# Tokens or features on the partitions: which operand of a split matrix product stays and which moves

## The chip, the cores and the metric

The program runs on one core of a Trainium2 chip. The metric is device time in microseconds (us) of one execution. TensorE (PE) multiplies a stationary operand, loaded first, by a moving operand that streams past it, into PSUM; VectorE (DVE), ScalarE (ACT) and GpSimd (POOL) work on tiles in SBUF and PSUM; SyncE (SP) issues nearly all loads of weights. Before the change the median of three runs is 2907.19 us (2906.72 to 2914.02).

## The reference, cut to what matters

256 tokens of width 1024 pass through two stacks, all in float32. First, twice:

```
x = layer_norm(a*x + 0.5*swiglu(x, ffn1_w1, ffn1_w2))     # 1024 -> 2 x 2816 -> 1024
x = layer_norm(a*x + token_mix(x))                        # three attentions, three gates, w_out
x = layer_norm(a*x + 0.5*swiglu(x, ffn2_w1, ffn2_w2))
...
swiglu(x, w1, w2):  gt, up = split(x @ w1);  return (silu(gt) * up) @ w2
token_mix:  g = sigmoid(h @ w_gate + b_gate)              # 1024 -> 3 x 1024
            merged = g0*(o_a @ w_br_a) + g1*(o_b @ w_br_b) + g2*(o_c @ w_br_c)
            return merged @ w_out
```

Then a state-space mixer (SSD) with layer norm, a mixture of 32 experts (two per token, hidden width 512) with layer norm, a dilated attention with layer norm, and a second such mixture with layer norm. That makes ten layer norms.

## The kernel before, in words

**Split products.** A float32 product is made of three fp32r products. Every weight tile of 128 x 1024 is split into a high part (`split`, L82, ACT) and the rest (L83, DVE), and so is the activation; `mm3` (L109 to L112) issues high x high, high x low and low x high. Such weights land in four raw tiles of 1 MB (`wraw`, tag w) and are split into a ring of seven tiles (`whl`, NSPLIT).

**Features on partitions.** x lies as `X["h"]`, `X["l"]` (the split parts) and `X["T"]` (whole), each [128 features, 8 chunks, 256 tokens]. In every split product a block of 128 x 128 weights is the stationary operand and the 256 tokens move, so the product has 128 features on the partitions, 256 tokens along the row.

**Stages.** `ffn` walks over 22 hidden chunks j of 128: `gate_up` projects gate and up (8 chunks of x, 24 products each), the activations are made on ACT and DVE, and `acc_second` adds chunk j - 2 to eight accumulators, four PSUM banks (24 products). `token_mix` projects queries, keys and values, runs attention a, then `branch_gate(0)` and `branch_out(0)`, the same for b and c, and w_out chunk by chunk behind the last branch (`done`). SSD and dilated attention end with an output product in the same form. A list scheduler orders the instructions of each engine: in program order where it can, but a later instruction that is ready fills a gap.

**Layer norm** (`finish`, L211): the last two or three chunks of the accumulation run output chunk by output chunk (`last_chunks`), and behind each of them DVE adds the residual (L230), subtracts a first mean (L234), ACT squares (L238), and PE sums over partitions with matrices of ones (L267, L268). Then follow variance, scale and shift for each chunk (L298 to L309). PE is given products of ones (`warm`, L198: ten of them, 20 records, four in the experts' norm) while it waits. `after_norm` orders the splits behind the norm's work.

**Experts** (`moe`): pairs of experts; tokens are gathered by a product with a selection matrix (L1459), gate and up (L1491) and down (L1527) have 64 gathered tokens stationary in half the columns of the array and 512 weight columns moving, unsplit fp32; the result is added back by L1555, eight products of 256 columns. An unsplit fp32 product of full width makes two records. Weights come straight from HBM into a ring of 21 tiles of 1 MB. The residual enters by products with a scaled unit matrix (L1301), x is turned to tokens on partitions (L1355), and the last pair's norm takes its mean ahead.

**Setup.** Parameter rows (norm weights, gate biases, SSD's) are loaded into three tiles `prow` out of two buffers and turned on PE (L159) during the first FFN.

Of the kernel before, what the change touches and what calls it, by code (L numbers as in the profile page):

```python
# [18 lines left out]
D = 1024  # L19
# [3 lines left out]
ORDER = ("a6 r r r r a5 a4 a3 s s s s s s s a2 a1 a0 x2 x0 x1", "a6 a5 r r r r a4 a3 a2 a1 a0 s s s s s s s x2 x0 x1")  # L23
GROUPED = {c: g for g in ((0, 1, 2, 3, 4, 5),) for c in g}
SETUPJ = (4, 10, 18)
POOLC = (6, 7)
MP, MD = (0, 1, 2, 3), (4, 5, 6)
# [3 lines left out]
WARM = 10  # L31
W2 = 4
W3 = 4
SC2 = 2
DTAIL = 2
F = 2816
# [10 lines left out]
def tile_stack(ctx: ExitStack, tc: tile.TileContext, a: dict, out: bass.AP):  # L47
# [20 lines left out]
    def after_norm(*ins):  # L68

        n = behind.get("n", 99)  # L70
        for k, x in zip(("act", "dve"), ins):
            if n < NSPLIT - TAIL and behind["known"]:
                tc.add_manual_dep(x.ins, behind[k + "0"].ins.name, order, reason="norm")
                if k == "dve":
                    tc.add_manual_dep(x.ins, behind["add0"].ins.name, order, reason="norm")
            elif NSPLIT - TAIL <= n < NSPLIT:
                tc.add_manual_dep(x.ins, behind[k].ins.name, order, reason="norm")
        behind["n"] = behind.get("n", 99) + 1

    def split(w, shape):  # L80
        hi, lo = split_tile(shape)
        after_norm(nc.scalar.activation(out=hi, in_=w, func=AF.Copy),  # L82
                   nc.vector.tensor_tensor(out=lo, in0=w, in1=hi.bitcast(F32), op=ALU.subtract))  # L83
        return hi, lo

    def acc_second(accs, c, n, wh, wl, mh, ml):
        for o in range(KC):
            mm3(accs[o // 2][:, o % 2, :], wh[:, o * 128:(o + 1) * 128], wl[:, o * 128:(o + 1) * 128], mh, ml,
                first=(c == 0 and o % 2 == 0), last=(c == n - 1), skip=True)

    def project_group(tiles, ws):

        for c in range(KC):
            for i, (wh, wl, n) in enumerate(ws):
                mm3(tiles[i // 2][0:n, i % 2, :], wh[:, c], wl[:, c], X["h"][:, c, :], X["l"][:, c, :],
                    first=(c == 0 and i % 2 == 0), last=(c == KC - 1), skip=True)
        return [tiles[i // 2][:, i % 2, :] for i in range(len(ws))]
# [11 lines left out]
    def mm3(o, wh, wl, xh, xl, first, last, skip=False):  # L109
# [10 lines left out]
    ones8 = const.tile([128, 128], F32)  # L120
    nc.vector.memset(ones8, 8.0 / D)

    prow = [
# [10 lines left out]
    pars = const.tile([128, 384], F32)  # L134

    def load_params(pp, pq):
# [6 lines left out]
        for i in range(3):  # L143
# [13 lines left out]
        for i in range(3):  # L157
# [3 lines left out]
        nc.vector.tensor_scalar(out=bg, in0=pars[:, pcol["b_gate"]:pcol["b_gate"] + 48].rearrange("p (l c) -> p l c", l=DEPTH),  # L161
                                scalar1=0.5, scalar2=None, op0=ALU.mult)

# [4 lines left out]
    bg = const.tile([128, DEPTH, 24], F32, name="bg")  # L168
# [5 lines left out]
    def x_tile(key, shape=(128, KC, S), dtype=F32R):  # L174

        return xp.tile(list(shape), dtype, tag="x" + key, name="x" + key)

    def new_x():
        X["h"], X["l"] = x_tile("h"), x_tile("l")
        if "T" not in X:  # L180
            X["T"] = x_tile("T", dtype=F32)
# [13 lines left out]
    def warm(out, n, after):  # L195

        for _ in range(n):
            x = nc.tensor.matmul(out=out, lhsT=ones, rhs=ones8.unsqueeze(1).to_broadcast([128, 2, 128]), start=True, stop=True,  # L198
# [3 lines left out]
    def last_chunks(accs, ks, first):  # L202

        def f(c):
            cs = slice(c * 128, (c + 1) * 128)
            for n, (wh, wl, mh, ml) in enumerate(ks):
                mm3(accs[c // 2][:, c % 2, :], wh[:, cs], wl[:, cs], mh, ml, first=(first and n == 0 and c % 2 == 0),
                    last=(n == len(ks) - 1), skip=True)
        return f

    def finish(accs, last, scale, g, b, write=None, loaded=False, mean=None, side="right"):  # L211

        with pool(name="lnps", bufs=1, space=PSUM, side=None if side else "right") as lps, pool(name="lnr", bufs=1, side=side) as lr, \
                pool(name="lnt", bufs=2, side=side) as tmp:
            rT = lr.tile([128, KC, S], F32, name="rT")  # L220
            st = lps.tile([128, 2, S], F32, name="lnst")
            sv = lps.tile([128, S], F32, name="lnsv")
            if not loaded:
                table("natural_log_exp_and_others")
            end, part, done = None, {}, []
            for c in range(KC):
                acc = accs[c // 2][:, c % 2, :]
                last(c)
                if mean is None:
                    nc.vector.scalar_tensor_tensor(out=rT[:, c, :], in0=X["T"][:, c, :], scalar=ALPHA * scale, in1=acc,  # L230
                                                   op0=ALU.mult, op1=ALU.add)
                    if c == 0:
                        nc.tensor.matmul(out=st[:, 0, :], lhsT=ones8, rhs=rT[:, 0, :], start=True, stop=True)
                    nc.vector.tensor_tensor(out=rT[:, c, :], in0=rT[:, c, :], in1=st[:, 0, :], op=ALU.subtract)  # L234
                else:
                    behind["dve0"] = nc.vector.tensor_tensor(out=rT[:, c, :], in0=acc, in1=mean, op=ALU.subtract)
                sq = tmp.tile([128, S], F32, tag="sq", name="sq", bufs=3)
                behind["act0"] = nc.scalar.activation(out=sq, in_=rT[:, c, :], func=AF.Square)  # L238
                if mean is not None:
                    eng, cs = (nc.gpsimd, MP) if c in MP else (nc.vector, MD if c in MD else (c,))  # L240
                    if c != cs[0]:
                        q2 = tmp.tile([128, S], F32, tag="q2" if c in MP else "r2", name="q2")
                        x = eng.tensor_tensor(out=q2, in0=part[cs], in1=sq, op=ALU.add)  # L243
                        if c in MD:
                            behind["add0"] = x
                        sq = q2
                    part[cs] = sq
                    if c == cs[-1]:
                        end = nc.tensor.matmul(out=sv, lhsT=ones, rhs=sq, start=(not done), stop=(c == KC - 1), skip_group_check=True)  # L249
                        done.append(c)  # L250
                    continue
                if c in GROUPED:
# [1525 lines left out]
```

## Time and profile before

| | |
|---|---|
| median of 3 runs | 2907.19 us |
| the profiled execution's own time | 2909.27 us |
| its span, first to last instruction | 2907.4 us |
| mean granted TensorE clock | 0.990 |
| bytes read from HBM | 693.25 MB |

In the rows below a time at the start of a line is us from the span's start. A line of the timeline shows start, duration, engine, source line, operation, what is written and read, stationary rows x columns, moving shape, and how many equal instructions were merged; what stands in brackets is idle time of the engine before it and what ended it. PE's instructions are pipelined: each is shown for longer than the distance to the next one's start, and that distance is what a product costs in a stream. In such lines a merged group's duration runs to the end of its last product.

### The profile page before, as it was taken

The page shows a single profiled execution, that of the slowest core. Times are in us where ns is not written, and L with a number is a line of the kernel's source. Part 1 is how long each engine was busy: PE and PEld are TensorE (multiplying, and loading weights), DVE is VectorE, ACT ScalarE, POOL GpSimd, SP SyncE. Part 2 cuts the span into 40 slices and gives each one's busy share as a digit, 9 for nine tenths or more (in the row PEclk, how much of TensorE's full clock was granted, in tenths as well). Part 3 has the DMA queues.
Part 4 walks back from the last instruction along what each step waited for, and adds up shares of the span by engine and source line. Part 5 has one row for each costly group of instructions (what it writes and reads, how often), then busy time and mean ns, then how long its engine had stood idle before and what let it go on. Part 6 is the DMA issues. An engine that isn't in the chain of part 4 may idle for free. (4 is left out here: it accounts for less than half of the span.)

```text
span 2907.4 us, 46673 instructions
## 1 busy us (share of the span) xinstructions
PE 2806.7 (97%) x19129; PEld 2194.8 (75%) x19129; DVE 1402.8 (48%) x3051; ACT 1069.7 (37%) x1985; POOL 196.1 (7%) x263
## 2 busy tenths in 40 slices
PE   8899999999999999999999989999998999999998
PEld 8798899999999889999988954445447974444444
DVE  5466665755755756575688741111118752111103
ACT  4344555544544455544467620101015531000002
POOL 2102000200200200020010010000002010000000
PEclk9899999999999999999999999999999999999999
DMA  8765454455455645445545579999956468999992
GB/s 225 194 203 149 134 154 145 145 194 189 155 179 161 179 118 163 145 147 191 167 133 192 220 309 416 421 421 421 421 230 181 132 232 328 421 421 421 421 421 98
DMA packets 312106, 697.45 MB, mean 240 GB/s; under 512 B 19460, under 2 KB 238384, under 8 KB 262736
## 3 DMA queue, kind: packets, MB, share of 16 engines
q1 hardware_dynamic: 300288, 677.62, 63.9%
q10 hardware_dynamic: 9296, 11.66, 1.4%
q0 software_dynamic: 2304, 5.15, 1.2%
q8 instruction: 152, 2.49, 0.4%
q14 instruction: 66, 0.54, 0.1%
HBM read 693.25 MB, written 4.27 MB: 240 GB/s over the span
## 5 line engine op out<-in xcount | busy, mean ns | idle before, releaser
L83 DVE TENSOR_TENSOR whl<-w,whl 128x1024 fp32r<-128x1024 f32 x487 | 591.2, 1220 | 348.8 <-ACT whl L82 343.3
L82 ACT ACTIVATE whl<-w 128x1024 fp32r<-128x1024 f32 x487 | 507.2, 1050 | 355.8 <-PE gu L112 106.6
L110 PE MATMUL pp<-xh,whl 128*128 128x256 f32 x1432 | 417.4, 292 | 9.7 <-DVE cv L935 4.7
L111 PE MATMUL pp<-xl,whl 128*128 128x256 f32 x1432 | 417.9, 292 | 1.1 <-DVE xl L307 1.0
L112 PE MATMUL pp<-xh,whl 128*128 128x256 f32 x1432 | 412.3, 288 | 0.4 <-DVE whl L509 0.4
L110 PE MATMUL gu<-xh,whl 128*128 128x256 f32 x1408 | 400.7, 285 | 4.0 <-DVE h L360 2.6
L112 PE MATMUL gu<-xh,whl 128*128 128x256 f32 x1408 | 400.7, 285 | 0.5 <-DVE whl L83 0.5
L111 PE MATMUL gu<-xl,whl 128*128 128x256 f32 x1408 | 400.8, 285 | 0.1
L110 PEld LDWEIGHTS pp<-xh,whl 128*128 128x128 f32 x1432 | 273.8, 191 | 18.1 <-ACT xh L306 5.7
L111 PEld LDWEIGHTS pp<-xl,whl 128*128 128x128 f32 x1432 | 274.5, 192 | 10.0 <-issue 6.9
L112 PEld LDWEIGHTS pp<-xh,whl 128*128 128x128 f32 x1432 | 274.2, 192 | 4.3 <-issue 2.4
L110 PEld LDWEIGHTS gu<-xh,whl 128*128 128x128 f32 x1408 | 272.0, 193 | 6.3 <-ACT whl L82 3.5
L111 PEld LDWEIGHTS gu<-xl,whl 128*128 128x128 f32 x1408 | 272.2, 193 | 0.8 <-DVE xl L307 0.7
L112 PEld LDWEIGHTS gu<-xh,whl 128*128 128x128 f32 x1408 | 272.1, 193 | 0.8 <-DVE whl L83 0.8
L110 PE MATMUL acc<-hhi,whl 128*128 128x256 f32 x704 | 201.6, 286 | 2.4 <-DVE rT L230 2.2
L111 PE MATMUL acc<-hlo,whl 128*128 128x256 f32 x704 | 200.1, 284 | 1.6 <-issue 1.6
L112 PE MATMUL acc<-hhi,whl 128*128 128x256 f32 x704 | 198.9, 284 | 0.0
L1509 DVE SCALAR_TENSOR_TENSOR t<-t,gps 128x512 f32<-128x512 f32 x32 | 22.0, 687 | 352.7 <-ACT t L187 352.7
L1459 PEld LDWEIGHTS xgp<-ot,xtok 128*128 128x128 f32 x1024 | 120.9, 191 | 50.3 <-issue 24.3
L1459 PE MATMUL xgp<-ot,xtok 128*128 128x128 f32 x1024 | 136.9, 283 | 15.8 <-ACT xg L1442 9.0
L110 PEld LDWEIGHTS acc<-hhi,whl 128*128 128x128 f32 x704 | 135.6, 193 | 5.4 <-DVE rT L230 4.0
L187 ACT ACTIVATE t<-gps 128x512 f32<-128x512 f32 x32 | 19.1, 597 | 320.8 <-PE gps L1491 320.8
(573 smaller groups left out, 4998.7 us busy)
## 6 DMA issues: line engine op xcount, KB each, us to landing
w<-in_ffn_w_dram SPq DMA_DIRECT2D x130, 1024.0 KB, 5.5
wa<-in_moe_w_up_dram SPq DMA_DIRECT2D x45, 1024.0 KB, 11.7
whl<-in_moe_w_down_dram SPq DMA_DIRECT2D x45, 1024.0 KB, 10.9
wa<-in_moe_w_gate_dram SPq DMA_DIRECT2D x44, 1024.0 KB, 12.5
whl<-in_moe_w_gate_dram SPq DMA_DIRECT2D x42, 1024.0 KB, 11.1
wa<-in_moe_w_down_dram SPq DMA_DIRECT2D x40, 1024.0 KB, 9.8
whl<-in_moe_w_up_dram SPq DMA_DIRECT2D x39, 1024.0 KB, 12.3
w<-in_w_in_dram SPq DMA_DIRECT2D x28, 1024.0 KB, 5.4
```

The source lines that it names most:

```text
L82: after_norm(nc.scalar.activation(out=hi, in_=w, func=AF.Copy), nc.vector.tensor_tensor(out=lo, in0=w, in1=hi.bitcast(F32), op=ALU.subtract))
L83: nc.vector.tensor_tensor(out=lo, in0=w, in1=hi.bitcast(F32), op=ALU.subtract))
L110: nc.tensor.matmul(out=o, lhsT=wh, rhs=xh, start=first, stop=False, skip_group_check=skip)
L111: nc.tensor.matmul(out=o, lhsT=wh, rhs=xl, start=False, stop=False, skip_group_check=skip)
L112: return nc.tensor.matmul(out=o, lhsT=wl, rhs=xh, start=False, stop=last, skip_group_check=skip)
L187: last_tanh.append(nc.scalar.activation(out=out, in_=in_, func=AF.Tanh, **kw))
L1459: ms.append(nc.tensor.matmul(out=ps[:, c, 0:P], lhsT=xt[:, i, (q * 4 + c) * 128:(q * 4 + c + 1) * 128], rhs=os[i], start=(i == 0), stop=(i ...
L1509: nc.vector.scalar_tensor_tensor(out=t[0:P], in0=t[0:P], scalar=1.0, in1=gps[0:P], op0=ALU.add, op1=ALU.mult)
```

## The change

Tokens go on the partitions for x and for nearly all products of weights with 512 columns; x itself stays in both forms: `X["k"]` [128 tokens, 2 halves, 1024] whole, and the split parts [128 features, 2 token halves, 8 chunks, 128 tokens].

- In FFN, branch gates, branch outputs, w_out, SSD's and the dilated attention's output, `mm3` gets a block of 128 features x 128 tokens as stationary operand and 512 weight columns as moving one. The other projections (queries, keys, values, SSD's input) keep their form.
- `ffn` works on 11 groups of two chunks with one PSUM tile `gu` of two banks (one buffer). Its gated activations have tokens on partitions, so four transposes for each group turn them (`turned`) behind the down product of group G - 2. In the first group the products run token half by token half.
- Gates and merged branches have tokens on partitions; `branch_gate(0)` stands ahead of attention a; the gate's bias is loaded as a broadcast tile and added on DVE; `done` turns the merged tile, four transposes for each quarter; w_out follows after the whole last branch.
- `finish`: the last chunks run by token half (`tail_half`), then for each half residual, `bn_stats`, `bn_aggr`, Ln and Exp on a column, scale and shift along the row with broadcast weights `gb`, and 8 transposes (`turn_x`). No products of ones are issued in it, and `after_norm` is gone.
- `moe`: no residual products, logits come out with tokens on partitions, x needs no turning, the add-back is four products of 512 columns, the last pair is treated as the others; the norm writes the output directly. The ring keeps 21 tiles (8 own ones, 2 of x in place of 7 and 3).
- Setup loads fewer parameter rows, into two `prow` tiles.

```diff
+    def acc_half(accs, t, wh, wl, mh, ml, first, last):
+        for hf in range(2):
+            hs = slice(hf * 512, (hf + 1) * 512)
+            mm3(accs[t][hf], mh[:, t * 128:(t + 1) * 128], ml[:, t * 128:(t + 1) * 128], wh[:, hs], wl[:, hs], first=first, last=last, skip=True)
+
     def acc_second(accs, c, n, wh, wl, mh, ml):
-        for o in range(KC):
-            mm3(accs[o // 2][:, o % 2, :], wh[:, o * 128:(o + 1) * 128], wl[:, o * 128:(o + 1) * 128], mh, ml,
-                first=(c == 0 and o % 2 == 0), last=(c == n - 1), skip=True)
+        for t in range(2):
+            acc_half(accs, t, wh, wl, mh, ml, first=(c == 0), last=(c == n - 1))
...
+    def tail_half(accs, ks):
+        def f(t):
+            for n, k in enumerate(ks):
+                acc_half(accs, t, *k, first=False, last=(n == len(ks) - 1))
+        return f
...
+    def turn_x(trp, t, hf, src, tag):
+        ps = trp.tile([128, 4, 128], F32, tag=tag, name="xps")
+        for c in range(4):
+            nc.tensor.transpose(ps[:, c, :], src[:, c * 128:(c + 1) * 128], ident)
+        cs = slice(hf * 4, hf * 4 + 4)
+        nc.scalar.activation(out=X["h"][:, t, cs, :], in_=ps, func=AF.Copy)
+        nc.vector.tensor_tensor(out=X["l"][:, t, cs, :], in0=ps, in1=X["h"][:, t, cs, :].bitcast(F32), op=ALU.subtract)
...
+            for t in range(2):
+                last(t)
...
+            for t in range(2):
+                st = tmp.tile([128, 2, 6], F32, tag="st", name="lnst")
+                for hf in range(2):
...
+                        nc.vector.scalar_tensor_tensor(out=r[:, t, hs], in0=k, scalar=ALPHA * scale, in1=accs[t][hf], op0=ALU.mult, op1=ALU.add)
+                    nc.vector.bn_stats(out=st[:, hf, :], in_=r[:, t, hs])
+                mv = tmp.tile([128, 2], F32, tag="mv", name="lnmv")
+                nc.vector.bn_aggr(out=mv, in_=st)
...
+                nc.scalar.activation(out=rs, in_=mv[:, 1:2], func=AF.Ln, bias=eps_t[scale], scale=1.0)
+                nc.scalar.activation(out=rs, in_=rs, func=AF.Exp, scale=-0.5)
...
+                nc.vector.scalar_tensor_tensor(out=r[:, t, :], in0=r[:, t, :], scalar=mv[:, 0:1], in1=gb[:, 0, :], op0=ALU.subtract, op1=ALU.mult)
+                nc.vector.scalar_tensor_tensor(out=nw, in0=mv[:, 1:2], scalar=eps_t[scale], in1=rs, op0=ALU.add, op1=ALU.mult)
...
+                for hf in range(2):
...
+                        nc.vector.scalar_tensor_tensor(out=k, in0=y, scalar=rs, in1=bias, op0=ALU.mult, op1=ALU.add)
+                    if write is not None:
+                        (nc.sync, nc.scalar)[hf].dma_start(out=write[t * 128:(t + 1) * 128, hs], in_=y)
+                    else:
+                        turn_x(trp, t, hf, k, tag)
...
+            def gate_up(G):
+                gu = gps.tile([128, 2, 512], F32, tag="gu", name="gu")
+                ws = []
+                for k in range(0, KC, 2):
+                    w = raw[G, k // 4][:, k % 4:k % 4 + 2].rearrange("p c i m -> p c (i m)")
+                    hi, lo = split(w, [128, 2, 512])
+                    ws += [(hi[:, i, :], lo[:, i, :]) for i in range(2)]
+                turns = [(k, t) for t in range(2) for k in range(KC)] if G == 0 else [(k, t) for k in range(KC) for t in range(2)]
+                for k, t in turns:
+                    mm3(gu[:, t, :], xh(k, t), xl(k, t), *ws[k], first=(k == 0), last=(k == KC - 1), skip=True)
+                return gu
+
+            def gating(gu):
+                e = tmp.tile([128, 2, 256], F32, tag="sg", name="sg", bufs=1)
+                tanh(out=e, in_=gu[:, :, 0:256], scale=0.5)
+                nc.vector.scalar_tensor_tensor(out=e, in0=e, scalar=1.0, in1=gu[:, :, 0:256], op0=ALU.add, op1=ALU.mult)
+                nc.vector.tensor_tensor(out=e, in0=e, in1=gu[:, :, 256:512], op=ALU.mult)
+                return e
+
+            def turned(G, e):
+                ps = trp.tile([128, 2, S], F32, tag="tr", name="hT")
+                for j in range(2):
+                    for t in range(2):
+                        nc.tensor.transpose(ps[:, j, t * 128:(t + 1) * 128], e[:, t, j * 128:(j + 1) * 128], ident)
...
+                e = gating(gate_up(G))
+                if G >= 2:
+                    for j, w in enumerate(down(G - 2)):
+                        acc_second(accs, 2 * (G - 2) + j, F // 128, *w)
+                turned(G, e)
+            ks = down(NG - 2) + down(NG - 1)
+            finish(accs, tail_half(accs, ks), 4.0, g, b, trp)
...
+            def branch_gate(r):
...
+                    pp = [pps.tile([128, 512], F32, tag="pp", name="pp") for t in range(2)]
+                    for k, t in ([(k, t) for t in range(2) for k in range(KC)] if r == 0 and hf == 0 else [(k, t) for k in range(KC) for t in range(2)]):
+                        mm3(pp[t], xh(k, t), xl(k, t), *ws[k], first=(k == 0), last=(k == KC - 1), skip=True)
+                    for t in range(2):
+                        o = gt[:, t, hf * 512:(hf + 1) * 512]
+                        nc.vector.tensor_tensor(out=o, in0=pp[t], in1=bias, op=ALU.add)
+                        tanh(out=o, in_=o, scale=0.5)
...
+                def combine(t):
+                    return [nc.tensor.matmul(out=accs[t][hf], lhsT=og[0:P, t * 128:(t + 1) * 128], rhs=ys[hf][0:P], start=first, stop=True,
+                                             skip_group_check=True) for hf in range(2)]
```

## Rows read from the trace of the kernel before

**Rows 1.** The page, busy time of each engine.
```profile
PE 2806.7 (97%) x19129; PEld 2194.8 (75%) x19129; DVE 1402.8 (48%) x3051; ACT 1069.7 (37%) x1985; POOL 196.1 (7%) x263
```

**Rows 2.** Windows: length, busy time (instructions) of each engine, granted clock, DMA share, GB/s.
```profile
560.00:740.00 180.00, 179.17 (x1487) 178.51 (x1486) 107.85 (x145) 83.68 (x113) 2.79 (x4) 1.00 0.57 193
1730.00:2150.00 420.00, 416.46 (x2130) 203.30 (x2132) 56.47 (x129) 39.18 (x72) 0.00 (x0) 1.00 1.00 413
2435.00:2860.00 425.00, 421.67 (x2152) 206.47 (x2152) 56.48 (x129) 40.27 (x73) 0.00 (x0) 1.00 0.98 407
```

**Rows 3.** Groups of PE's instructions by line and shape: count, busy us, mean ns.
```profile
L110 PE MATMUL gu<-xh,whl 128*128 128x256 f32 x1408 | 400.7, 285 | 4.0 <-DVE h L360 2.6 <-ACT whl L82 1.2
L110 PE MATMUL acc<-hhi,whl 128*128 128x256 f32 x704 | 201.6, 286 | 2.4 <-DVE rT L230 2.2
...
L110 PE MATMUL pp<-oh,whl 128*128 128x256 f32 x192 | 54.9, 286 | 1.0 <-DVE gt L779 1.0
...
L110 PE MATMUL sacc<-yh,whl 128*128 128x256 f32 x128 | 36.4, 291 | 1.1 <-DVE rT L230 1.1
```

**Rows 4.** Timeline of PE, gate and up of the first FFN.
```profile
102.68 0.28 PE L112 MATMUL gu<-xh,whl 128*128 128x256 f32 x1
...
103.40 0.28 PE L112 MATMUL gu<-xh,whl 128*128 128x256 f32 x1
```

**Rows 5.** Timeline of PE, a projection with 32 weight columns stationary.
```profile
1002.40 0.28 PE L112 MATMUL pp<-xh,whl 128*32 128x256 f32 x1
...
1003.19 0.28 PE L110 MATMUL pp<-xh,whl 128*32 128x256 f32 x1
```

**Rows 6.** Timeline of PE: short fp32 products, add-back of the experts, transposes.
```profile
1004.22 1.86 PE L673 MATMUL sc<-kcz,qa 128*128 128x30 f32 x16
...
2502.02 3.72 PE L1555 MATMUL eacc<-og,y 128*128 128x256 f32 x16
2505.58 0.38 PE L1475 MATMUL ogp<-ident,ogt 128*128 128x128 f32 x2
...
2521.66 0.64 PE L1512 MATMUL htp<-ident,t 128*128 128x128 f32 x4
```

**Rows 7.** Groups of DVE's and ACT's instructions by line and shape.
```profile
L83 DVE TENSOR_TENSOR whl<-w,whl 128x1024 fp32r<-128x1024 f32 x484 | 590.0, 1225 | 348.8 <-ACT whl L82 343.3 <-DMA posi<-in_positions_dram 0.5
...
L1510 DVE TENSOR_TENSOR t<-t,ups 128x512 f32<-128x512 f32 x32 | 22.0, 687 | 66.0 <-PE ups L1491 66.0
...
L1539 ACT ACTIVATE y<-yp 128x512 f32<-128x512 f32 x60 | 35.8, 597 | 254.7 <-PE yp L1527 254.7
```

**Rows 8.** Timeline of PE around the first norm, after an FFN.
```profile
227.90 0.28 PE L112 MATMUL acc<-hhi,whl 128*128 128x256 f32 x1
...
235.75 5.19 PE L198 MATMUL acc<-ones,ones 128*128 128x256 f32 x20
241.09 0.36 PE L110 MATMUL pp<-xh,whl 128*128 128x256 f32 x1
```

**Rows 9.** Timeline of PE around the norm after the dilated attention.
```profile
2379.44 0.28 PE L112 MATMUL dacc<-oh,whl 128*128 128x256 f32 x1
...
2388.48 0.34 PE L1305 MATMUL lgp<-xh,rs 128*72 128x256 f32 x1
```

**Rows 10.** Windows, the stretch behind the first mixture's norm.
```profile
2196.00:2206.00 10.00, 8.20 (x32) 6.93 (x32) 10.00 (x20) 4.79 (x10) 8.72 (x8) 0.52 0.07 18
```

**Rows 11.** Timeline of PE, just ahead of that stretch.
```profile
2190.07 1.89 PE L198 MATMUL eacc<-ones,ones 128*128 128x256 f32 x8
```

**Rows 12.** Timeline of PE, setup in the first FFN.
```profile
114.30 0.45 PE L159 MATMUL ptr<-ident,prow 128*128 128x128 f32 x1 [9.06 <-DMA prow<-in_ssd_norm_w_dram]
```

**Rows 13.** The chain that ended last, in order of time: start, us, what.
```profile
2877.74 5.38 PE yp L1527 x24
...
2895.43 0.44 DVE nw L284
...
2899.33 2.12 DMA out_dram<-oc
```

More of the change, by code (lines that the diff above doesn't have):

```diff
@@ L197, in warm @@
         for _ in range(n):
-            x = nc.tensor.matmul(out=out, lhsT=ones, rhs=ones8.unsqueeze(1).to_broadcast([128, 2, 128]), start=True, stop=True,
+            x = nc.tensor.matmul(out=out, lhsT=ones, rhs=ones.unsqueeze(1).to_broadcast([128, 2, 128]), start=True, stop=True,
                                  skip_group_check=True)
             tc.add_manual_dep(x.ins, after.ins.name, order, reason="clock")
[L202 to L222, printed above, removed]
+    def spread(ap):
+        return ap.unsqueeze(0).to_broadcast([128, ap.shape[0]])
@@ new lines, in by_rows, with finish @@
+    def by_rows(ap):
+        return ap.rearrange("p (k f) -> p f k", k=4)
+    def finish(accs, last, scale, g, b, trp, tag="tr", room=None, dealt=False, was_dealt=False, write=None, loaded=False):
+        with pool(name="lnt", bufs=2) as tmp, ExitStack() as own:
+            if room is not None:
+                room = own.enter_context(pool(name="lnr", bufs=1, side=room))
+                gb = room.tile([128, 2, D], F32, name="gb")
+                r = room.tile([128, 2, D], F32, name="lnx")
+            else:
+                gb = raw_tile([128, 2, D], "gb")
+                r = X["k"]
+            for i, p in enumerate((g, b)):
+                nc.sync.dma_start(out=gb[:, i, :], in_=spread(p))
@@ L223, in finish @@
             if not loaded:
                 table("natural_log_exp_and_others")
[L225 to L252, printed above, removed]
-                    first = c == GROUPED[c][0]
-                    if first:
-                        rsum, qsum = rT[:, c, :], sq
-                    else:
-                        r2 = tmp.tile([128, S], F32, tag="r2", name="r2")
-                        nc.vector.tensor_tensor(out=r2, in0=rsum, in1=rT[:, c, :], op=ALU.add)
-                        q2 = tmp.tile([128, S], F32, tag="q2", name="q2")
-                        nc.gpsimd.tensor_tensor(out=q2, in0=qsum, in1=sq, op=ALU.add)
-                        rsum, qsum = r2, q2
-                    if c != GROUPED[c][-1]:
-                        continue
-                else:
-                    rsum, qsum = rT[:, c, :], sq
-                begin = c <= GROUPED[0][-1]
-                nc.tensor.matmul(out=st[:, 1, :], lhsT=ones, rhs=rsum, start=begin, stop=(c == KC - 1))
-                end = nc.tensor.matmul(out=sv, lhsT=ones, rhs=qsum, start=begin, stop=(c == KC - 1))
@@ L1079, in ssd @@
             st3.close()
[L1080 removed]
+            trp = st.enter_context(pool(name="strp", bufs=2, space=PSUM))
+            finish(accs, tail_half(accs, tail), 1.0, g, b, trp, room="left", dealt=True, loaded=True)
     def dilated(g_, b_):
@@ L1494, in run @@
                 phase(*ms)
-                if last:
-                    nc.vector.tensor_copy(out=sums, in_=accs[0][:, 0, :])
-                    for c in range(1, KC):
-                        nc.vector.tensor_tensor(out=sums, in0=accs[c // 2][:, c % 2, :], in1=sums, op=ALU.add)
-                    ps = mp.tile([128, S], F32, tag="m", name="meanp")
-                    nc.tensor.matmul(out=ps, lhsT=ones, rhs=sums, start=True, stop=True)
-                    nc.scalar.activation(out=mean, in_=ps, func=AF.Copy)
                 t = wk.tile([128, HID], F32, tag="t", name="t", bufs=1)
@@ L1658, in moe @@
                     steps = (first_half, lambda hold=hold: hold["steps"][1]())
-                last = run(xg, ogs, ld, 2, q == NP - 1, steps)
+                combine = run(xg, ogs, ld, 2, steps)
+                if q < NP - 1:
+                    add(combine)
                 if q < NP - 1:
```

494 lines of the change are left out of this document (178 added, 316 removed), and 5 rows, old and new, of the table prow.

## The prediction

> **What bounds the kernel now.** First the page: PE is busy 97% of the span, DVE 48%, ACT 37% [rows 1]. Then windows by stage: inside an FFN PE is busy 179 of 180 us at granted clock 1.00 while DMA moves 193 GB/s [rows 2], so PE alone sets the time there. In both mixtures PE is busy 99% too, but DMA stands at 0.98 to 1.00 of its time and 407 to 413 GB/s [rows 2]: two limits at once. "Busy" doesn't say that PE works at its peak, so the timeline comes next: six products of gate and up start 0.72 us apart, one every 0.120 us [rows 4]. At the granted clock of 1.00 (the 2.4 GHz level) 256 columns at one per cycle are 0.1067 us; 0.0133 us, 11%, is paid for each instruction. Last the norms: from the last product of the first FFN to the first product that uses its norm 13.2 us pass, in which PE sums, waits and multiplies ones [rows 8]; behind the dilated attention 9.0 us [rows 9]. Nine such gaps (the first and one late one are shown; the tenth norm ends the kernel) are 6.7 to 13.2 us long and 83 us in all.
>
> **The width, the main term.** Products that change form: four FFNs give 3 x 1408 for gate and up and 3 x 704 for down; the outputs of branches 3 x 192; SSD 3 x 128 [rows 3]; w_out again 384, the dilated attention 96 and the gates 1152 (3 x 8 x 8 products, 3 branches, 2 layers; in the trace part of a larger group). Sum 8928, which become 4464 of 512 columns; the columns streamed stay the same. What one of these costs no row shows. Streaming alone: 0.2133 us, the lower end. If the 0.0133 us come once for each instruction: 0.2267, the upper end. Two rows lie nearer. With only 32 weight columns stationary the same 256 moving columns take 0.79/7 = 0.113 us [rows 5]: half of the overhead goes with the length of the weight load, and sixteen short products with full loads follow at 1.86/16 = 0.116 us at most [rows 6], so a load fits under a product of 0.213 us, not under one of 0.107. What stays is 0.006 us: 0.2195 us. The experts' add-back streams 512 columns per record (two passes of 256) with a full load and takes 3.56/16 = 0.2225 [rows 6]. I take 0.2195: (0.240 - 0.2195) x 4464 = **-92 us**; with the row of the add-back -78, bounds -119 and -59.
>
> The Trainium skill ("TensorE: Matmul & The Clock Gate", Back-to-back issue gap) gives N/2.4 + 2.5 ns for an isolated product. By that 256 columns would take 0.109 us, and the trace disagrees with 0.120 [rows 4]; by its 0.2157 us for 512 columns the term would be -108 us.
>
> **Transposes added.** 44 for each FFN, 16 in each token mix: 208 in PE's stream. Four merged ones take 0.64 us with the last one's drain [rows 6], a short product with a full load 0.116; at 0.12 each **+25 us** (bounds 24 and 33). Their copies to `hhi` and `hlo` replace as many as before, in 512-wide pieces.
>
> **Waits in the FFN.** `gu` has one buffer, so the next group's products wait until ACT and two passes of DVE have read it: 0.60 + 2 x 0.69 [rows 7] and some 0.3 us of hand-over, 2.3 us. From group 2 on the down product of G - 2 (24 x 0.22 = 5.3 us) hides that, and also a split that stands ahead on ACT or DVE (at most 1.2 us). Groups 0 and 1 have no down product: 8 waits in four FFNs, **+19 us** (with a split ahead +29). Without that cover everywhere 36 more waits would show, a rival below. Splits per group stay six; DVE has 6 x 1.23 + 3 x 0.69 = 9.4 us of work in a group in which PE has 16.3, so DVE doesn't become the bound.
>
> **Waits in the token mix.** Both `pp` tiles end together and are freed only by DVE's additions of 0.69 us [rows 7]: about 1 us at each of 12 half gates, **+12 us**. Nothing, if attention fills them; and up to 35, since attention a loses its filler: `branch_gate(0)` stood behind it and could fill its gaps with eight chunks of 2.9 us; now later projections have to. The bias DMAs go on ACT's queue and are small.
>
> **The norms.** DVE carries the new norm alone. For each half: residual 2 x 0.69, `bn_stats` 2 x 0.69 (no row; between nothing and the 1.23 of a double-width pass; taken as one pass of 512), `bn_aggr` and three column operations 0.8 (at most 0.44 each [rows 13], taken at 0.2), one pass of 1024 at 1.23 that hides Ln and Exp on ACT, then twice scale-and-shift and low part, 2.75: 7.5 us, 15.0 for both, 15.5 with hand-overs. PE has under it the second half's tail (24, 12, 18 or 12 products behind FFN, mix, SSD, dilated attention: 5.3, 2.6, 4.0, 2.6 us; 0.9 behind experts) and, where the next stage starts by halves, its first half (5.3 in FFN and gate, 1.9 in the router). What is left open: two FFN-to-mix and one FFN-to-FFN 4.9, two mix-to-FFN 7.6, FFN-to-SSD 10.2, SSD-to-experts 9.6, dilated-to-experts 11, experts-to-dilated 14.6: 75 against 83 now, and a split of 1.23 us that slips in between on DVE's queue with `after_norm` gone, nine times 11: **+3 us**. The 8 transposes per half run in these gaps. `gb` is loaded by SP: in FFN and mix into a raw tile that is free about 10 us ahead; behind SSD and dilated attention it shares DMA with the experts' weights, and a late `gb` moves the whole norm (bound +10).
>
> **Experts, end, setup.** The pair itself stays: 16 records of 0.2225 become 8 of about 0.43, and DMA is as close a limit as PE. Ahead of the routing the turned logits, the turning of x and its copies, and the residual products go: -4 for each mixture, **-8** (bounds 0, since DMA is near, and -16). The end: now 24.3 us pass from the last down product (2883.1, start plus duration [rows 13]) to the span's end; then 0.6 of copy, 0.9 of add-back, 12.3 of DVE (15.0 without the four low parts) and a store of 2.1 [rows 13], with hand-overs 17.5: **-7**. In setup PE stands 9.1 us for the third `prow` tile [rows 12], which now isn't there, and works slowly just behind it: **-11**.
>
> **The clock.** In the stretch behind the experts' norm the granted clock is 0.52, near the 1.2 GHz level, and PE is busy 8.2 of 10 us [rows 10]: about 4 us of loss. Ahead of it PE had little but eight records of ones [rows 11]. Behind the norms with 20 records [rows 8] it is better: the FFN's window, which begins 12 us behind its norm, shows 1.00 [rows 2]. The new norms issue none. Behind FFN PE has work most of the time; the longer gaps may drop. Four more drops: **+16** (bounds 0 and eight drops, +32).
>
> **Sum.** -92 + 25 + 19 + 12 + 3 - 8 - 7 - 11 + 16 = -43. From the profiled execution's own 2909.3: 2866; it lies 2 us above the median, so **2864 us**.
>
> **Rivals.** (1) The overhead comes once per instruction: 0.2267, term -59: 2897, hardly faster. For: all full-width rows show 0.0133. Against: the row with 32 columns. Chance 0.15. (2) Slower: fp32r with full weights streams at 0.120 per 256 columns, 0.240 per 512. Then the width gives nothing: 2864 + 92 = 2956. It decides from about 0.2300 us on, where the term no longer pays the other +49. Against it speaks [rows 5]. Chance 0.09. (3) The single `gu` shows in every group, because splits stand ahead of the gating in the strict queues of ACT and DVE: 36 x 2.3 = +83, 2947. Against: 5.3 us of cover. Chance 0.08. (4) The clock drops behind all norms: +16, 2880. For: it did so where PE had little to do [rows 10, 11], and nothing but transposes runs in the new gaps. Chance 0.10. The Trainium skill (same page, PE-mode transpose) says that transposes don't count as activity for the clock; no run here shows it, as transposes now stand among products. That the change does nothing is excluded: the instruction count falls by thousands.
>
> **How the numbers follow.** Forecast 0.58, within 2820 to 2890, all but 0.02 of it faster by over 0.3% (8.7 us, about what a measurement of this kernel can tell from no change). (1): 0.08 faster, 0.05 same, 0.02 slower; (2) slower; (3) 0.07 slower, 0.01 same; (4) 0.07 faster, 0.03 same. Faster 0.71, same 0.11, slower 0.18. Low end: no drop of the clock (-16), filled gates (-12), half of the way to the width's lower bound (-13) and no splits in the norms (-11) with the router's bound (-8), less 4 since not all come together: 2808. High end: (1) with the gates' bound (+23): 2920.
>
> **What would show it.** Right: `gu` and `acc` products 0.217 to 0.223 us apart at clock 1.00; FFN windows near 185 us between norms; two stalls of 2.3 us at the head of each FFN; norm gaps of 5 to 15 us with DVE busy through; the stall at L159 gone. Wrong: a step of 0.227 or more, a wait for `gu` in later groups, clock near 0.5 behind most norms, or attention a with PE idle.

## The result, and the profile after

The changed kernel takes 2876.39 us (median of 4 runs, 2874.72 to 2883.18) against 2908.85 (median of 4): ratio 0.9890, 95% interval 0.9869 to 0.9912. That is 32 us less, where 43 were forecast, and 12 us above the predicted time. The profiled execution has a span of 2873.7 us, 33.7 less than before.

First the page of the changed kernel, busy time of PE, PEld, DVE, ACT and POOL, and then windows: the second FFN and a stretch of each mixture (columns as in [rows 2]).

```profile
PE 2721.6 (95%) x14368; PEld 1890.8 (66%) x14368; DVE 1345.2 (47%) x2669; ACT 991.6 (35%) x1699; POOL 57.9 (2%) x124
```

```profile
550.00:736.00 186.00, 183.53 (x833) 151.49 (x832) 103.31 (x105) 82.15 (x92) 0.00 (x0) 1.00 0.57 181
...
1720.00:2130.00 410.00, 407.00 (x1979) 178.25 (x1980) 55.70 (x126) 37.63 (x68) 0.00 (x0) 1.00 1.00 417
2420.00:2820.00 400.00, 397.00 (x1934) 172.80 (x1930) 54.50 (x123) 37.24 (x67) 0.00 (x0) 1.00 1.01 421
```

PE has 4761 instructions less and is busy 85 us less [rows 1], but its share fell from 97 to 95%: it waits more. The mixtures still stand at two limits, as in [rows 2].

The step of the wide products, from the timeline of PE (start, duration; the first at the granted clock of 1.00, the last two in the stretch behind the norm of the token mix):

```profile
554.11 0.39 PE L117 MATMUL gu<-whl,xh 128*128 128x512 f32 x1
...
555.47 0.39 PE L117 MATMUL gu<-whl,xh 128*128 128x512 f32 x1
```

```profile
547.34 0.63 PE L116 MATMUL gu<-whl,xh 128*128 128x512 f32 x1
547.77 0.63 PE L117 MATMUL gu<-whl,xh 128*128 128x512 f32 x1
```

Six steps in 1.36 us are 0.2267 us each, where the products of 256 columns took 0.120 [rows 4]. At the low level a step takes 0.43, which is 512 columns at one per cycle of 1.2 GHz (0.427).

The norms. Behind the first FFN (timeline of PE; in brackets what ended the wait):

```profile
226.42 0.39 PE L118 MATMUL acc<-whl,hlo 128*128 128x512 f32 x1
228.81 1.50 PE L181 MATMUL xps<-ident,xk 128*128 128x128 f32 x8 [2.00 <-DVE xk L263]
230.12 0.79 PE L116 MATMUL pp<-whl,xh 128*128 128x512 f32 x1
```

3.7 us pass from the last product to the first that uses the norm, against 13.2 [rows 8]; the first half's norm runs under the second half's products. Behind the token mix it is 8.9 us: the tail there is shorter, a split stands ahead of the first half's scaling in DVE's queue, and on ACT a load of the activation table (1.28 us) stands ahead of the first half's copies (timeline of all engines):

```profile
540.70 1.22 DVE L66 TENSOR_TENSOR whl<-w,whl 128x1024 fp32r<-128x1024 f32 x1
541.84 1.41 DVE L263 SCALAR_TENSOR_TENSOR xk<-xk,lnrs,gb 128x512 f32<-128x512 f32 x2
...
543.95 1.28 ACT L194 ACT_TABLE_LOAD   x1
...
545.25 1.09 ACT L183 ACTIVATE xh<-xps 128x512 fp32r<-128x512 f32 x2
...
545.89 0.80 PE L116 MATMUL gu<-whl,xh 128*128 128x512 f32 x1 [1.22 <-ACT xh L183]
```

All nine gaps: 3.7, 8.9, 3.7, 3.9, 8.9, 11.8, 4.7, 13.1 and 11.8, together 70 against 83.

The granted clock behind the norms fell. Over the ten us that begin with the next stage's first product it is 1.00 behind one norm, 0.77 to 0.92 behind six and 0.50 behind the two ahead of a mixture; in the kernel before it was 1.00 behind eight and 0.53 behind one. Here behind the first token mix and ahead of the first mixture, then behind the same token mix in the kernel before (columns as in [rows 2]):

```profile
546.00:556.00 10.00, 10.00 (x39) 8.04 (x40) 4.17 (x8) 1.53 (x3) 0.00 (x0) 0.77 0.37 113
1668.00:1678.00 10.00, 8.56 (x40) 7.82 (x38) 6.64 (x13) 3.57 (x6) 0.00 (x0) 0.50 1.01 420
```

```profile
548.50:558.50 10.00, 9.98 (x80) 9.67 (x80) 10.00 (x21) 4.84 (x9) 9.89 (x8) 1.00 0.01 2
```

Over the whole span the mean granted clock is 0.970, where it was 0.990.

Two waits are new (timeline of PE). In each FFN the first group's gating stands open, here in the second FFN; and in the first FFN PE stands 14.4 us ahead of the transposes of a later group, while the wait for the third parameter tile [rows 12] is gone:

```profile
562.63 0.63 PE L317 MATMUL hT<-ident,sg 128*128 128x128 f32 x4 [2.46 <-DVE sg L310]
```

```profile
91.90 1.11 PE L317 MATMUL hT<-ident,sg 128*128 128x128 f32 x4 [14.39 <-DVE sg L310]
```

And attention a, whose filler now runs ahead of it: windows of 58 us in the kernel before and 70 us in the changed kernel.

```profile
290.00:348.00 58.00, 57.95 (x414) 46.73 (x413) 38.59 (x181) 34.98 (x106) 1.66 (x5) 1.00 0.44 119
```

```profile
306.00:376.00 70.00, 63.83 (x373) 46.67 (x373) 45.27 (x190) 36.67 (x107) 1.65 (x5) 0.90 0.37 111
```

PE was busy throughout; now it is idle for 6 us of 70, and the granted clock is 0.90.

### The profile page after: what moved, and what is told of

Same layout as the page of the kernel before. It is cut to its first block, busy times and chain, and to the rows that moved or that the text cites. A ratio compares the mean times of both kernels' runs of the same rounds, so it can differ in the third digit from the quotient of the medians.

```text
span 2873.7 us, 36446 instructions
## 1 busy us (share of the span) xinstructions
PE 2721.6 (95%) x14368; PEld 1890.8 (66%) x14368; DVE 1345.2 (47%) x2669; ACT 991.6 (35%) x1699; POOL 57.9 (2%) x124
## 5 line engine op out<-in xcount | busy, mean ns | idle before, releaser
L116 PE MATMUL pp<-xh,whl 128*128 128x256 f32 (+1 forms) x1048 | 301.4, 288 | 4.8 <-DVE cv L909 3.2
L117 PE MATMUL pp<-xl,whl 128*128 128x256 f32 (+1 forms) x1048 | 302.9, 289 | 0.0
L118 PE MATMUL pp<-xh,whl 128*128 128x256 f32 (+1 forms) x1048 | 298.7, 285 | 0.0
L116 PE MATMUL gu<-whl,xh 128*128 128x512 f32 x704 | 284.3, 404 | 4.3 <-ACT xh L183 2.4
L117 PE MATMUL gu<-whl,xh 128*128 128x512 f32 x704 | 279.6, 397 | 0.8 <-DVE whl L66 0.8
L118 PE MATMUL gu<-whl,xl 128*128 128x512 f32 x704 | 279.7, 397 | 0.3 <-DVE xl L184 0.3
L116 PEld LDWEIGHTS pp<-xh,whl 128*128 128x128 f32 (+1 forms) x1048 | 199.0, 190 | 11.4 <-issue 5.1
L117 PEld LDWEIGHTS pp<-xl,whl 128*128 128x128 f32 (+1 forms) x1048 | 199.0, 190 | 3.4 <-issue 1.7
L118 PEld LDWEIGHTS pp<-xh,whl 128*128 128x128 f32 (+1 forms) x1048 | 198.8, 190 | 1.8 <-issue 0.9
L116 PEld LDWEIGHTS gu<-whl,xh 128*128 128x128 f32 x704 | 135.5, 192 | 32.8 <-ACT xh L183 3.8
L118 PEld LDWEIGHTS gu<-whl,xl 128*128 128x128 f32 x704 | 135.2, 192 | 31.2 <-DVE xl L184 1.6
L117 PEld LDWEIGHTS gu<-whl,xh 128*128 128x128 f32 x704 | 135.3, 192 | 28.3 <-DVE whl L66 1.1
L116 PE MATMUL acc<-whl,hhi 128*128 128x512 f32 x352 | 137.3, 390 | 0.0
L118 PE MATMUL acc<-whl,hlo 128*128 128x512 f32 x352 | 137.1, 389 | 0.0
L117 PE MATMUL acc<-whl,hhi 128*128 128x512 f32 x352 | 137.0, 389 | 0.0
## 6 DMA issues: line engine op xcount, KB each, us to landing
wa<-in_moe_w_down_dram SPq DMA_DIRECT2D x44, 1024.0 KB, 11.8
```

Source lines behind the costliest of these rows:

```text
L116: nc.tensor.matmul(out=o, lhsT=wh, rhs=xh, start=first, stop=False, skip_group_check=skip)
L117: nc.tensor.matmul(out=o, lhsT=wh, rhs=xl, start=False, stop=False, skip_group_check=skip)
L118: return nc.tensor.matmul(out=o, lhsT=wl, rhs=xh, start=False, stop=last, skip_group_check=skip)
```

## The experiments

Each is the changed kernel with one edit, unless said. Times are medians; ratios are against the kernel before on the same chip, to be held against 0.9890.

**e1_width: the width alone undone.**

```
+        if xh.shape[-1] == 512:
+            for k, (w, x) in enumerate(((wh, xh), (wh, xl), (wl, xh))):
+                for q in range(2):
+                    qs = slice(q * 256, q * 256 + 256)
+                    m = nc.tensor.matmul(out=o[:, qs], lhsT=w, rhs=x[:, qs], ...)
```

> The changed kernel with every 512-column product cut into two of 256 columns again, all else as it is: 4464 products become 8928. Theory A (at the full clock 13.3 ns are paid once for each instruction, whatever its length): 4464 x 0.0133 = +59 us, about 2935 us. Rival B (the change is worth more than its products, as wider moves also give the splits and loads more room): over +75 us. Rival C (part of the width's gain is taken up by later waits and never comes to the end): under +45 us.

Measured: 2919.70 us, ratio 1.0032 (1.0020 to 1.0045), 43 us more. The products take 0.120 us again, 59 us more in all, so 16 of the 59 never came to the end: rival C. They are found by stage (from last product to last product of the stages). The first FFN is only 4.3 us longer, not 10.5 (792 x 0.0133): the 240 products ahead of the 14 us wait are free, since that wait ends when transfers land, and it ended 1.2 us sooner in this run (at 90.7 us). The FFNs behind a token mix are 7.2 and 6.1 us longer, as the gap ahead of them is 5.1 us in place of 8.9: in this run neither the split on DVE (1.2 us) nor the table load on ACT (1.28 us) stands ahead of the first half's scaling and copies. That is another order of the same work by the scheduler, and not the width itself; the tail of 12 products is longer by only 12 x 0.0133 = 0.16 us. The two token mixes are 5.2 and 5.0 us longer, not 7.0 (528 x 0.0133).

**e5_steps: the step by itself**, products alone (one execution). Timeline of PE, one line for each shape (start, from first start to last end, stationary rows x columns, moving columns):

> Only products, none of the reference's computation: 64 fp32r products in a row for each of 12 shapes (128, 96, 64 or 32 weight columns stationary, 512, 256 or 128 columns moving), then 32 fp32 products each with 128 or 32 stationary and 512 or 256 moving. Read is the step from one product to the next at the full clock. Theory A (a cost of each instruction that goes with the loaded columns and is never hidden): 512 columns take 0.2267 with 128 stationary and about 0.220 with 32, each 256-column step 0.1067 below its 512-column one. Theory B (the cost is the same for every load under a long product; only short products show the load): 0.2267 at 512 for all four loads, and with 128 columns moving a step far above 0.0667 for 128 stationary. The prediction's step (a load is hidden under a product of 0.213 us): 0.2195 at 512 columns for 128 stationary, which the changed kernel has already answered with 0.2267.

```profile
40.02 14.67 PE L57 MATMUL r128by<-xh 128*128 128x512 f32 x64
54.53 14.89 PE L57 MATMUL r96by<-xh 128*96 128x512 f32 x64
69.25 14.87 PE L57 MATMUL r64by<-xh 128*64 128x512 f32 x64
83.97 14.99 PE L57 MATMUL r32by<-xh 128*32 128x512 f32 x64
98.79 7.83 PE L57 MATMUL r128by<-xh 128*128 128x256 f32 x64
...
121.13 7.42 PE L57 MATMUL r32by<-xh 128*32 128x256 f32 x64
128.39 7.26 PE L57 MATMUL r128by<-xh 128*128 128x128 f32 x64
135.48 5.61 PE L57 MATMUL r96by<-xh 128*96 128x128 f32 x64
...
144.76 4.01 PE L57 MATMUL r32by<-xh 128*32 128x128 f32 x64
148.61 27.68 PE L57 MATMUL f128by<-xk 128*128 128x512 f32 x64
...
217.81 14.00 PE L57 MATMUL f32by<-xk 128*32 128x256 f32 x64
```

Less the last one's duration (0.39, 0.28, 0.27; for 128 columns with 96 and 32 stationary 0.25 and 0.22) and over 63 steps: 512 columns take 0.2267 us with 128 stationary columns, and no less with 96, 64 or 32 (0.230 to 0.232). 256 columns take 0.120 with 128 stationary and 0.1133 with 32, which is half of 0.2267. 128 columns take 0.111 with 128 stationary, 0.085 with 96 and 0.060 with 32. So theory A falls; of theory B both signs are there, the first within 0.005 us. The load of 128 columns shows under 256 columns (0.0067 us) and not under 512. What is left is not one cost for each instruction: over one column per cycle at 2.4 GHz it is 0.0067 us at 256 columns and 0.0133 at 512, both 0.4427 ns for each column, 6% over. At 128 columns this line gives 0.0567, and 0.060 was measured, so it isn't shown to hold there; what the 6% are made of stays open. Records of fp32 with 512 and with 256 columns (0.59 and 0.38 us for the last one) take 0.430 and 0.216 us, both some 0.003 over two cycles per column. So the 6% belong to fp32r, and what fp32 pays does not grow with the columns.

**e2_router and e8_dcol: the wait in the first FFN.** In the changed kernel the split of the router's weights, which ran at 1472.6 us before, runs inside the first FFN, and ACT waits for its load (timeline of ACT):

```profile
85.61 0.44 ACT L1246 ACTIVATE rs<-rw 128x288 fp32r<-128x288 f32 x1 [21.59 <-DMA rw<-moe_w_router_expert_dram]
```

The first edit orders this split behind the last FFN:

```
+            behind["ffn"] = list(marked)
...
+        for x, y in zip((nc.scalar.activation(out=rs[:, :, 0:36], in_=rw[:, l], func=AF.Copy),
...
+                        behind["ffn"]):
+            tc.add_manual_dep(x.ins, y.ins.name, order, reason="router")
```

> The changed kernel with the split of the router's weights on ACT and DVE ordered behind the last FFN instead of wherever it fits (it ran 85.6 us into the first FFN, after ACT had waited 21.6 us for its DMA). Theory A: that wait alone holds the gating of the first FFN's sixth group, so the stall of 14.4 us ahead of the transposes at 91.9 us goes, and with it 1.8 us at the low clock: -14 to -17 us, about 2861 us. Rival B: the setup's own loads are late as they were before (9.1 us at the third parameter tile), the stall only moves to the next of them: -5 us or less.

Measured: 2878.39 us, ratio 0.9892 (0.9877 to 0.9907): no change. ACT now waits just as long for the FFN's own weights (timeline of ACT in this run):

```profile
86.66 2.00 ACT L65 ACTIVATE whl<-w 128x1024 fp32r<-128x1024 f32 x2 [22.32 <-DMA w<-in_ffn_w_dram]
```

So theory A falls; all loads were late together. Windows of 3 us of the changed kernel show it (last two columns: DMA share, GB/s): from 65 to 77 us nothing moves, though the queues are not empty.

```profile
62.00:65.00 3.00, 3.00 (x15) 2.48 (x14) 1.47 (x2) 1.06 (x1) 2.77 (x4) 1.00 2.29 18
65.00:68.00 3.00, 3.00 (x15) 2.49 (x14) 0.28 (x1) 0.00 (x0) 0.00 (x0) 1.00 0.00 0
68.00:71.00 3.00, 3.00 (x15) 2.46 (x14) 0.00 (x0) 0.00 (x0) 0.00 (x0) 1.00 0.53 0
71.00:74.00 3.00, 3.00 (x15) 2.49 (x14) 0.00 (x0) 0.00 (x0) 0.75 (x1) 1.00 2.29 1
```

Just ahead of it POOL issues two loads of 4 KB each that fetch single numbers (dcol, 17.4 us to landing). The second edit loads whole rows:

```
-        d = a["ssd_d_2"][0].rearrange("(j t) -> t j", t=2)
-        for t in range(2):
-            nc.gpsimd.dma_start(out=dcol[t * 64:t * 64 + 64], in_=d[t].unsqueeze(0).to_broadcast([64, 16]))
+        nc.gpsimd.dma_start(out=drow, in_=a["ssd_d_2"].to_broadcast([128, 32]))
```

> The changed kernel with the small parameter d of SSD loaded as one row of 32 numbers to each partition and picked apart on DVE, in place of two DMAs that fetch every second number by itself for 64 partitions each (dcol). Theory A: these two DMAs, which land 17.4 us after their issue (median), are what holds every transfer from about 64 to 79 us, the FFN's weights among them (24 us to landing); without them the stall of 14.4 us in the first FFN goes, and the 1.8 us at the low clock behind it: -13 to -17 us, about 2861 us. Rival B: another small load of the setup holds the queues (the router's weights, in pieces of 4 numbers), and the stall stays: within 3 us of no change.

Measured: 2860.43 us, ratio 0.9828 (0.9815 to 0.9841), -16 us, and the wait of 14.4 us is gone (the first FFN ends at 207.6 us, not 226.4). One of the same windows in this run:

```profile
71.00:74.00 3.00, 3.00 (x15) 2.49 (x14) 2.96 (x4) 1.83 (x3) 0.00 (x0) 1.00 0.97 385
```

Theory A holds. The Trainium skill ("DMA: Bandwidth & Descriptors", the rule on a strided last dim) says that such a load becomes one descriptor per element. The hold fits that (17.4 us to landing, in the median, for 4 KB), but no row here counts descriptors. That such loads also stop the other queue is shown by these rows alone.

**e10_before_dcol: the same edit in the kernel before.**

> The kernel before with the same edit of the load dcol. Theory A: the hold of the transfers is there too (76 to 94 us) but was almost covered by weights already at hand (PE stood 1.9, 1.6 and 0.9 us in the 35 us behind it, and 9.1 us for the third parameter tile, which goes on): -2 to -6 us, about 2904 us. Rival B: the wait for the third parameter tile was also an effect of the hold, which pushes all later loads: -10 us or more. Rival C: covered wholly: within 2 us of no change.

Measured: 2897.97 us against 2908.95, ratio 0.9961 (0.9949 to 0.9973), -11 us: rival B. The third parameter tile is there as before, and its wait fell from 9.06 us [rows 12] to 1.9 (timeline of PE in this run):

```profile
103.21 0.30 PE L159 MATMUL ptr<-ident,prow 128*128 128x128 f32 x1 [1.89 <-DMA prow<-in_ssd_norm_w_dram]
```

**e6_gu1: the second group in the accumulators.**

```
-                gu = gps.tile([128, 2, 512], F32, tag="gu", name="gu")
+                gu = gps.tile([128, 2, 512], ...) if G != 1 else [accs[t][0] for t in range(2)]
```

> The changed kernel with the second group's gate and up products of each FFN written into two of the accumulators, which lie idle until the third group. Theory A: the first group's gating is then hidden under them, so the four waits of 3.65, 2.63, 3.71 and 2.62 us behind the first group go, and with three of them 5 us at the low clock behind them: -11 to -17 us, about 2862 us. Rival B: the wait comes back at the third group, or the accumulators' own first products wait for the second group's gating: between -4 and +2 us.

Measured: 2861.23 us, ratio 0.9837 (0.9824 to 0.9851), -15 us, theory A. The gating of this group runs half by half. The one wait for DVE that the second FFN showed is gone; its transposes now stand between products. Where the third FFN's wait was, the granted clock over ten us is 1.00 (756 to 766 us) in place of 0.83 (758 to 768 us in the changed kernel).

**e3_filler and e3b_half: the filler of attention a.** In the first the whole `branch_gate(0)` goes back behind attention a, in the second only its second half (this diff):

```
-            gt = branch_gate(0)
+            gt = branch_gate(0, hfs=(0,))
...
+            branch_gate(0, gt, (1,))
             branch_out(0, a["w_br_a"][l], True, oh, ol, gt)
```

> The changed kernel with the whole gate of branch a put back behind attention a, where it stood before the change. Theory A: attention a's waits (2.63 + 1.30 + 1.83 us in the first token mix, 3.10 + 1.30 + 1.79 us in the second, 12 us together) go, as the gate's products fill them, but both norms ahead are then open until both halves of x are there, 9 us in place of 3.7 and 3.9: +10 us. Sum about -2 us, 2874 us. Rival B: the waits have another cause and stay: +10 us, 2886 us.

> The changed kernel with the second half of branch a's gate alone behind attention a; the first half stays ahead, under the norm's second half. Theory A (attention a lost its filler): most of its 12 us of waits go and the norms stay covered: -8 to -12 us, about 2866 us. Rival B (the waits are not for want of products): within 3 us of no change.

Measured: 2868.76 us, ratio 0.9860 (0.9842 to 0.9878), -8 us, and 2857.65 us, ratio 0.9820 (0.9803 to 0.9836), -19 us. Theory A both times, 6 and 7 us better than the expected ends. Attention a in the second run (windows):

```profile
300.00:370.00 70.00, 69.22 (x431) 53.45 (x430) 47.57 (x179) 40.19 (x107) 1.65 (x5) 1.00 0.44 128
```

PE is busy 5.4 us more in the same 70 us, and the granted clock is 1.00 in place of 0.90. The expectation had counted the waits and not the clock. In the first run the gap ahead of the token mix opens again, to a wait of 7.4 us on the second half, as expected.

**e4_hold: the splits in the last pair of experts.** In the first mixture PE stands 4.58 us ahead of the last pair's transposes (0.91 in the second, which no stage follows), because splits of the dilated attention's weights stand in DVE's queue. The edit orders the first five behind that pair's gating:

```
+            tc.add_manual_dep(x.ins, behind["tanh"].ins.name, order, reason="pair")
+            tc.add_manual_dep(y.ins, behind["hT"].ins.name, order, reason="pair")
```

> The changed kernel with the first five splits of the dilated attention's weights held back: on DVE behind the last expert pair's copy of hT, on ACT behind that pair's Tanh. Theory A: splits whose weights land late stand ahead of the last pair's gating in DVE's strict queue (gap of 5.2 us ahead of the transposes and 2.6 us ahead of the down products, against 1.5 and 1.1 us in the second mixture, where no stage follows, and then some 2 us of down products at the low clock): -6 to -8 us, about 2869 us. Rival B: the splits held back come out in the norm or ahead of the first projection: between -2 and +2 us.

Measured: 2876.87 us, ratio 0.9883 (0.9868 to 0.9898): rival B. The wait goes (0.82 us) and comes back in the norm: three splits now stand between its passes on DVE, and the transposes of the second half wait 4.69 us, where it was 1.20 (timeline of PE in this run):

```profile
2155.19 0.75 PE L1445 MATMUL htp<-ident,t 128*128 128x128 f32 x4 [0.82 <-DVE t L1443]
...
2183.19 1.94 PE L185 MATMUL xps<-ident,xk 128*128 128x128 f32 x8 [4.69 <-DVE xk L267]
```

**e7_warm: products of ones behind the norms.**

```
+                junk = trp.tile([128, 4, 128], F32, tag=tag, name="junk")
+                warm(junk[:, 0:2, :], {4.0: 4, 2.0: 10}.get(scale, 14 if was_dealt else 6), lastmm)
```

> The changed kernel with products of ones (256 columns, fp32) behind each norm's last product: 4 behind an FFN, 10 behind a token mix, 6 behind SSD and the dilated attention, 14 behind the experts, in the gaps in which TensorE waits. Theory A: the granted clock is then high when the gap ends; behind the norms of the changed kernel the steps at the low level cost 0.8, 1.8, 0.8, 1.4, 1.0, 0.5 and 0.9 us: -4 to -7 us, about 2871 us. Rival B: the products end after the gap or don't lift the clock: 0 to +5 us.

Measured: 2879.27 us, ratio 0.9895 (0.9879 to 0.9911): no gain. They do lift the clock: behind the first token mix it is 1.00 over the ten us from 546 on, in place of 0.77, and the FFN's second product lasts 0.40 us in place of 0.63. The FFN's first product comes 7.0 us after the last of the mix, not 8.9; in this run ACT's table load also comes behind the first half's copies, so how much of the 1.9 us is the clock's is not shown. But the dilated attention's stage is 3.7 us longer and SSD's 2.0, so the sum is nothing. What lengthens those two was not traced further.

**e9_all: three edits together** (e6, e3b, e8).

> The changed kernel with three of the edits together: the second group's gate and up in the accumulators (-15.2 us alone), the second half of branch a's gate behind attention a (-18.7 us alone) and the load dcol as whole rows. Theory A: the three lie in different stages and add up: -34 us and what the load gives alone, about 2828 us if that is 14. Rival B: the first FFN's stall and its first group's wait share cover, and a third of the sum is lost: about 2843 us.

Measured: 2820.63 us, ratio 0.9695 (0.9683 to 0.9708), -56 us, no less than the sum of the three alone (-50); the 6 us between are not clear of noise, as each interval is some 4 us to either side. Theory A. It beats both kernels: 3.0% less than before, where the change as made brought 1.1%.

## Why the prediction was nearly right, by its own steps

The time lies in the range and in the likeliest case's own (2820 to 2890). But the sum came out by errors that cancel, and that is luck. Of the prediction's own signs of being wrong, attention a with PE idle is there, the step (0.2267) stands at its mark of 0.227, and the granted clock fell behind eight of nine norms, near 0.5 over ten us behind two. Term by term, from the rows of the changed kernel:

| term | predicted | measured | from |
|---|---|---|---|
| width | -92 | -59 | 4464 x 0.0133; 43 of it reach the end |
| transposes | +25 | +23 | 208 x 0.11 |
| waits for `gu` | +19 | +11 | 3.65, 2.63, 3.71, 2.62, less 1.5 before |
| token mix | +12 | +12 | 5.8 and 6.2 in attention a |
| norms | +3 | -13 | gaps 70 against 83 |
| routing | -8 | -4 | first routing to first expert 25.3 and 21.1, before 25.2 twice |
| end | -7 | -6 | 17.0 from the end of the last down product, 22.6 before |
| setup | -11 | +5 | e8 16, e10 11 |
| clock | +16 | +8 | steps of the split products of 1.55 to 2.15 times their usual length, in stretches granted 0.5: what they have over it is 14 us, 6 before |
| other long steps | none | -11 | the same lengths where the granted clock is 1.00: 17 us, 28 before; their cause was not traced |

The measured column adds up to -34, and the span fell by 33.7. The rows were read one by one and can overlap (16 of the 59 of the width did not reach the end), so that the sum comes so close is partly chance.

- **The width: the step that failed.** "What stays is 0.006 us: 0.2195 us." The first half of the argument was right: half of the 0.0133 goes with the load of 128 columns and vanishes under a product of 512 (e5: 0.120 against 0.1133, and 2 x 0.1133 is 0.2267). The other half was taken as paid once per instruction. It doubles from 256 to 512 columns. So the step is 0.2267, the upper bound, and rival (1)'s condition came true for another reason than it gave: it had the whole 0.0133 once per instruction. Its 2897 was not reached because the norms (16 us), the other long steps (11), the clock and the waits for `gu` (8 each) came out lower, against 16 more for the setup. The row of the add-back [rows 6] was fp32, which streams without the 6%; it was the wrong neighbour for fp32r.
- **The norms** were priced too high by 16 us. The gaps came out at 70 us with the splits that stand in them, where 75 had been worked out without, and 11 more added for splits.
- **The clock** had four new drops at 4 us. More came, at the head of the stages: the granted clock fell behind eight of the nine norms, which is nearly the condition of rival (4). But they are cheap: the expectation of e7 read 0.5 to 1.8 us behind each of seven, and the split products lost 8 us more than before in all stretches granted 0.5. So the price per drop was too high, and rival (4)'s +16 over the forecast did not come.
- **The setup** was mis-signed. The row [rows 12] said what PE waited for, not why it was late: the load was held up with all others, by one that nobody waited for. With the tile gone, the same hold met the FFN's weights.
- **The end** rests on a reading that is 1.7 us off: the chain [rows 13] leaves the down products after 24 of 32, and the last one ends at 2884.8, not 2883.1 (timeline of PE, kernel before):

```profile
2884.23 0.59 PE L1527 MATMUL yp<-w,hT 128*64 128x512 f32 x1
```

- **Token mix and `gu`.** The half gates cost next to nothing; the 12 us came by the way that was named as the bound, the lost filler. Undone, filler and `gu` bring 19 and 15 us, more than their waits (12 and 13), and the granted clock comes back too (attention a 0.90 to 1.00, behind the third FFN's wait 0.83 to 1.00). The second group's wait for `gu` did not show: the scheduler put down products of the first group there. Rival (3) did not come.

## What to carry to other kernels

Before paying for a wider form, measure the step of that data type and both lengths alone: only the part of the overhead that does not grow with the columns is saved, and a row of another type does not tell it. When a term is undone to price it, compare the order of the instructions too: the scheduler put them down otherwise in e1, and some us of its difference are that. Where a wait names a DMA, look whether all queues stood still at that time, and for the small load issued just ahead: removing the wait that it caused only moves it. A stage that fills another's gaps is worth its waits and the clock behind them; half of it can often stay where it covers a norm.

## What the runs showed of the hardware

- fp32r products stream at 0.4427 ns per column at the granted clock of 1.00 (0.2267 us for 512, 0.1133 for 256; 128 took 0.060, above that line), and at one per cycle at the 1.2 GHz level (0.43 for 512). The Trainium skill ("TensorE: Matmul & The Clock Gate", Back-to-back issue gap) has 2.5 ns over the columns for an isolated product at the full clock. For fp32r the rows differ (13.3 ns over at 512, 6.7 at 256); for fp32 they nearly agree (about 3 ns over two cycles per column for records of 512 and of 256 columns).
- With 128 columns moving, the stationary ones show in the step of fp32r: it is 0.111 us with 128 of them and 0.085 with 96; with 64 and with 32 it is 0.060.
- Two loads of 4 KB that fetch single numbers held every transfer of the core for about 12 us (0 to 1 GB/s from 65 to 77 us) and cost 16 us at the end in one kernel and 11 in the other.
